# Convolution stage of a two-block transformer kernel: two alternating modulation accumulators, their column sums later, and another order of products in the first seven-product unit

## Chip, cores and metric

The kernel runs on one core of one Trainium2 chip. The metric is the device time of one execution, in microseconds (us). Engines are called PE (TensorE), ACT (ScalarE), DVE (VectorE), POOL (GpSimd) and SP (SyncE, which here only issues DMAs).

## What is computed

Two transformer blocks follow each other on 1024 rows of 1024 features, all in fp32. The first has attention and a mixture of experts. The second begins with a short convolution and ends with a gated feed forward. Only the second block's front is touched here:

```python
def second_block(x, c, ada_w, ada_b, norm_gains, conv_w_in, conv_w, conv_w_out, ...):
    c_act = jax.nn.silu(c)
    mod = c_act @ ada_w[i] + ada_b[i]                       # 6 vectors of 1024
    sh_m, sc_m, g_m, sh_f, sc_f, g_f = jnp.split(mod, 6, axis=-1)
    h = modulate(rms_norm_2(x, norm_gains[i, 0]), sh_m, sc_m)
    h = short_conv_mixer(h, conv_w_in[j], conv_w[j], conv_w_out[j])
    x = x + g_m[:, None, :] * rms_norm_2(h, norm_gains[i, 1])
    h = modulate(rms_norm_2(x, norm_gains[i, 2]), sh_f, sc_f)
    h = swiglu(h, ffn_w_gate_up[i], ffn_w_down[i])
    return x + g_f[:, None, :] * rms_norm_2(h, norm_gains[i, 3])

def short_conv_mixer(h, w_in, w_conv, w_out):
    gate_b, gate_c, v = jnp.split(h @ w_in, 3, axis=-1)
    u = gate_c * v
    conv = causal convolution of u over 3 rows, per feature
    return (gate_b * conv) @ w_out
```

The vector `mod` has 12 halves of 512 columns. Halves 0 to 3 (`sh_m`, `sc_m`) are made early in the kernel. Halves 4 to 11 (`g_m`, `sh_f`, `sc_f`, `g_f`) are made during the convolution stage, beside the product `h @ w_in`.

## The kernel before

Every fp32 operand of a matmul is split into a high and a low part (a cast on ACT, a subtraction on DVE, lines 79 and 80), and three matmuls (lines 239 to 241) make one product of the split operands.

**Seven-product units.** After a first stretch in the common form, `h @ w_in` is done in units of 256 weight columns by Winograd's form of Strassen's product (`wino`, L1538): seven products, each of 4 x 3 matmuls, called by what the weights multiply: 11, T2, T3, T1, 21, T4, 22. The weights of 11, T2, T3 and T1 are the split pair `g1` (`w_one`), those of 21, T4 and 22 the pair `g2` (`w_two`). The sums of weight blocks that they need are made on POOL (`w_sums`, L1516 to L1519). A unit's raw weights are one DMA of 1 MB (`cwraw`, issued on SP at L225). A product lands in one PSUM bank of seven (tag `pb`); ACT copies 11 (`p1c`, L1563), and DVE adds the others up (L1561). In two units of three POOL and DVE also multiply the result with an earlier factor (L1647, L1649). The row differences T1, T2, T3 are made by `wino_t` (L1479), T4 by `wino_t4`. The convolution stage has nine such units. The feed forward calls the same function for twenty units.

**Modulation beside it.** `ada_conv` (L1582) makes the eight halves in 64 steps (8 halves of 8 steps k). A step loads 256 KB of `ada_w` by a DMA on SP (L1589), scales it on ACT in place (L1597; for k = 0 into the accumulator), and adds it to the accumulator on POOL (L1599; not for k = 0). The tile `adt` (in the traces `s_st`) has four slots of 512 columns: three for raw rows, one for the accumulator. So the load of step n + 2 may go out when step n - 1 has left its slot, and the step k = 0 of the next half must wait until the column sums of the last half have read the accumulator. These column sums (`ada_finish`, L172) are four small matmuls on PE (L175) and an add on DVE (L179). In program order each product starts one step (`ada_step`, L1555), or two for 11 and 21: nine in a unit.

**Order of the work.** The program's order is a priority. A planner (the framework's scheduler, with a timing model of its own) places each instruction on its engine when it finds it ready; after that every engine, and SP's queue, is strictly in order. In the trace PE's column sums stand between matmuls 6 and 7 (twice 7 and 8) of T2, and not where the program writes them.

**After the stage.** The raw rows for the output projection (`yr`, L1683, loaded from `y_d`) take the memory of `adt`, so their load waits on SP for the last column sums. Their split (into the memory of `hh`, `hl`, which the nine units read until their end) feeds the first matmuls of the output projection (`pm`).

Of the kernel before, what the change touches and what calls it, by code (L numbers as in the profile page):

```python
# [45 lines left out]
def block_kernel(ctx: ExitStack, tc: tile.TileContext, a, out, dbg=None, upto=99):  # L46
# [35 lines left out]
    # ---------------------------------------------------------------- constants  # L82
# [18 lines left out]
    def newton_rsqrt(eng, v, n, name, iters=3):  # L101
        """rsqrt(-2v) of v < 0: y = y*(1.5 + v*y*y)"""
# [23 lines left out]
    def rstd_s(ss, n, name):  # L126
        """as rstd_of, from the square root of ACT"""
# [20 lines left out]
    # ---------------------------------------------------------------- adaptive modulation  # L148
# [4 lines left out]
    def ada_gen(pool_, which, h, eng, tags="ad"):  # L153
        """One 512-column half of the modulation vector, in steps."""
# [26 lines left out]
    # ---------------------------------------------------------------- DRAM scratch  # L181
# [25 lines left out]
    def build_h(t, src, rstd, arow, brow, tmp, hi, lo, eng=None):  # L207
        """h = src*rstd*arow + brow, transposed into the split halves of token tile t."""
        h_rows(t, src, rstd, arow, brow, tmp.tile([P, D], F32, name="hrow", tag="hrow", bufs=hb[0]), hi, lo, eng)
# [33 lines left out]
    # ================================================================ phase 1: z  # L243
# [77 lines left out]
    # shift and scale, the same row in every partition  # L321
# [25 lines left out]
    def ada_start(items):  # L347
        """the halves in turn on DVE and on ACT with Pool"""
# [23 lines left out]
    def rope(dst, src, t, nb):  # L372
        """dst, src [P, nb, 64]"""
# [10 lines left out]
    def put(hi, lo, src, scale=1.0):  # L384
        """the split halves of scale*src"""
# [3 lines left out]
    def rope4(t, pz, hi, lo, scale):  # L389
        """four rope heads of 64, transposed in pairs into the split tiles"""  # L390
# [9 lines left out]
    def ct_chunk(t, pz, hi, lo):  # L400
        """rms of the 256 columns of pz, transposed into the split tiles"""
# [103 lines left out]
    for i, (kind, c) in enumerate(chunks):  # L505
# [6 lines left out]
        if i == 1:  # L512
            # the rest of the modulation waits for the up projections
# [53 lines left out]
    # ================================================================ phase 2: attention  # L567
# [140 lines left out]
    def gate_w(raw, c):  # L708
        """gate1 goes into the columns of the projection"""
# [61 lines left out]
    # ================================================================ phase 3: out projection, router  # L771
# [80 lines left out]
    # the router works on the unnormalised row: logits = rstd*(x1 @ (a2*wr)) + (s2 @ wr + br)  # L852
# [14 lines left out]
    def router(t, xT, r):  # L867
# [43 lines left out]
        # tokens and weights of the slots, by rank and expert  # L911
# [63 lines left out]
    # the rows of ys_d that hold a token's two results: its slots, or the row of zeros if the expert was full  # L975
# [606 lines left out]
    def ada_conv():  # L1582
# [10 lines left out]
        for n_, (h, k) in enumerate(steps):  # L1593
# [7 lines left out]
            if k == KD - 1:  # L1601
                ada_finish(adt[:, 3, :], 1, h)
# [417 lines left out]
```

## Time and profile before

| What | us |
| --- | --- |
| median of three runs | 2591.1 |
| lowest and highest run | 2588.51 and 2593.97 |
| span of the profiled execution, first to last instruction | 2593.1 |
| PE busy in it | 2367.3 (91%) |
| DVE, ACT, POOL busy | 1916.8 (74%), 1213.2 (47%), 1034.5 (40%) |

The profiled execution's own time is not listed apart from its span; the span lies 2.0 us above the median of the runs and within what they cover. All times of rows are counted from the start of that span. The convolution's seven-product units run from 1572.5 to 1785.8 us, the feed forward's from about 1947 us on. A busy share is an average; what a stage is worth is read from who waits for whom in that stage.

### The profile page before, as it was taken

The page shows a single profiled execution, that of the slowest core. Times are in us where ns is not written, and L with a number is a line of the kernel's source. Part 1 is how long each engine was busy: PE and PEld are TensorE (multiplying, and loading weights), DVE is VectorE, ACT ScalarE, POOL GpSimd, SP SyncE. Part 2 cuts the span into 40 slices and gives each one's busy share as a digit, 9 for nine tenths or more (in the row PEclk, how much of TensorE's full clock was granted, in tenths as well). Part 3 has the DMA queues.
Part 4 walks back from the last instruction along what each step waited for, and adds up shares of the span by engine and source line. Part 5 has one row for each costly group of instructions (what it writes and reads, how often), then busy time and mean ns, then how long its engine had stood idle before and what let it go on. Part 6 is the DMA issues. An engine that isn't in the chain of part 4 may idle for free. (4 is left out here: it accounts for less than half of the span.)

```text
span 2593.1 us, 35011 instructions
## 1 busy us (share of the span) xinstructions
PE 2367.3 (91%) x12889; PEld 1955.1 (75%) x12889; DVE 1916.8 (74%) x2965; ACT 1213.2 (47%) x1622; POOL 1034.5 (40%) x973
## 2 busy tenths in 40 slices
PE   6998889999898899999999688899998999999986
PEld 3888768888798577766666577778986888887775
DVE  7777457777667799999999586676687555558777
ACT  3344346666522577766677443444232222223443
POOL 2644115554512221232520466883343333437143
PEclk8999999999999899999999689999998999999999
DMA  7566983331435799999998743445212222137545
GB/s 283 160 220 191 294 264 107 114 105 51 141 125 185 266 382 379 379 381 366 375 372 323 206 132 111 149 142 167 98 66 78 68 91 89 66 114 243 171 146 171
DMA packets 253379, 503.74 MB, mean 194 GB/s; under 512 B 21009, under 2 KB 99089, under 8 KB 248849
## 3 DMA queue, kind: packets, MB, share of 16 engines
q1 hardware_dynamic: 236210, 436.69, 48.7%
q0 software_dynamic: 16704, 63.71, 8.5%
q8 instruction: 102, 1.67, 0.3%
q10 hardware_dynamic: 288, 1.05, 0.1%
q14 instruction: 75, 0.61, 0.1%
HBM read 427.46 MB, written 78.13 MB: 195 GB/s over the span
## 5 line engine op out<-in xcount | busy, mean ns | idle before, releaser
L1039 DVE TENSOR_TENSOR mlo<-mraw,mhi 128x1024 fp32r<-128x1024 f32 x378 | 440.2, 1216 | 28.9 <-ACT mhi L1034 13.7
L1034 ACT CAST mhi<-mraw 128x2048 fp32r<-128x2048 f32 (+1 forms) x193 | 364.0, 1903 | 72.6 <-PE gu L241 27.8
L240 PE MATMUL gu<-mlo,xh 128*96 128x512 f32 x512 | 206.0, 402 | 10.6 <-DVE mlo L1039 10.6
L239 PE MATMUL gu<-mhi,xh 128*96 128x512 f32 x512 | 203.6, 398 | 0.0
L241 PE MATMUL gu<-mhi,xl 128*96 128x512 f32 x512 | 201.0, 393 | 0.0
L1043 POOL DMA_INDIRECT xg<-h_d,idxg x32 | 120.4, 3761 | 100.2 <-PE xT L1054 87.2
L241 PE MATMUL pz<-zhi,hlo 128*128 128x256 f32 (+1 forms) x512 | 149.7, 294 | 6.6 <-DVE hlo L80 6.6
L239 PE MATMUL pz<-zhi,hhi 128*128 128x256 f32 (+1 forms) x512 | 148.8, 295 | 7.4 <-ACT zhi L79 7.3
L1105 POOL DMA_DIRECT2D ys_d<-ysb x30 | 16.2, 541 | 336.2 <-DVE ysb L1103 329.6
L240 PE MATMUL pz<-zlo,hhi 128*128 128x256 f32 (+1 forms) x512 | 149.1, 293 | 0.6 <-DVE zlo L80 0.6
L601 PE MATMUL ps<-k,oq 128*128 128x512 f32 x416 | 127.4, 418 | 15.2 <-ACT em L608 9.7
L239 PE MATMUL wm<-hh,g2hi 128*128 128x512 f32 x348 | 135.4, 389 | 0.0
L240 PE MATMUL wm<-hl,g2hi 128*128 128x512 f32 x348 | 135.4, 389 | 0.0
L241 PE MATMUL wm<-hh,g2lo 128*128 128x512 f32 x348 | 135.4, 389 | 0.0
L606 DVE TENSOR_REDUCE nmx<-ps 128x1 f32<-128x1024 f32 x96 | 116.1, 1218 | 22.7 <-PE ps L601 22.3
L240 PE MATMUL dd<-pp 128*128 128x512 f32 x308 | 121.5, 396 | 8.9 <-DVE pp L80 8.7
L241 PE MATMUL dd<-pp 128*128 128x512 f32 x308 | 119.7, 390 | 0.0
L240 PEld LDWEIGHTS gu<-mlo,xh 128*96 128x96 f32 x512 | 82.8, 162 | 46.3 <-DVE mlo L1039 14.9
L79 ACT CAST pp<-dr 128x1024 fp32r<-128x1024 f32 x55 | 57.5, 1050 | 128.3 <-POOL dr L1852 50.1
L239 PE MATMUL dd<-pp 128*128 128x512 f32 x308 | 108.9, 396 | 8.7 <-ACT pp L79 4.5
L80 DVE TENSOR_TENSOR ptwraw<-pT,ptwhi 128x512 fp32r<-128x512 f32 x128 | 83.9, 682 | 36.9 <-ACT ptwhi L79 36.8
L239 PEld LDWEIGHTS gu<-mhi,xh 128*96 128x96 f32 x512 | 82.9, 162 | 36.3 <-ACT mhi L1034 1.2
(604 smaller groups left out, 7487.6 us busy)
## 6 DMA issues: line engine op xcount, KB each, us to landing
mraw<-in_w_expert_gate SPq DMA_DIRECT2D x64, 1024.0 KB, 16.5
mraw<-in_w_expert_up SPq DMA_DIRECT2D x64, 1024.0 KB, 17.1
mraw<-in_w_expert_down SPq DMA_DIRECT2D x64, 1024.0 KB, 15.2
fwraw<-in_ffn_w_gate_up SPq DMA_DIRECT2D x21, 1024.0 KB, 5.7
dr<-a_d SPq DMA_DIRECT2D x77, 256.0 KB, 4.3
adraw<-in_w_ada SPq DMA_DIRECT2D x64, 256.0 KB, 4.1
s_st<-in_ada_w SPq DMA_DIRECT2D x64, 256.0 KB, 2.9
dr<-in_ffn_w_down SPq DMA_DIRECT2D x55, 256.0 KB, 4.3
```

The lines of the kernel that those rows point to most:

```text
L79: act.copy(hi, src)
L80: (eng or dve).tensor_tensor(out=lo, in0=src, in1=f32(hi), op=OP.subtract)
L239: pe.matmul(ps, lhsT=lh, rhs=rh, start=first, stop=False)
L240: pe.matmul(ps, lhsT=lh, rhs=rl, start=False, stop=False)
L241: pe.matmul(ps, lhsT=ll, rhs=rh, start=False, stop=last)
L601: pe.matmul(ps[:, cs], lhsT=l, rhs=r[:, cs], start=(i == 0), stop=(i == len(passes) - 1))
L606: dve.reduce_max(nm, ps, axis=AX.X, negate=True)
L1034: act.copy(hi[:, m], raw[:, m])
L1039: eng.tensor_tensor(out=lo[:, m], in0=raw[:, m], in1=f32(hi[:, m]), op=OP.subtract)
L1043: pool.indirect_dma_start(out=xg[e % XG][:CAP], out_offset=None, in_=h2f, in_offset=bass.IndirectOffsetOnAxis(ap=idxg[:CAP, e:e + 1], axis=0),
L1105: (sp if e >= NE - 2 else pool).dma_start(ys_d[e * CAP:(e + 1) * CAP, :], y)
```

## The change

Two things are changed, and a number of comments are taken out.

First, `ada_conv`: `adt` has the same four slots, now two for raw rows and two for accumulators that alternate between halves. A step loads one step ahead where it loaded two ahead, so the load of step n + 1 may go out when step n - 1 has left its slot. The column sums of a half are written after the step k = 4 of the following half; those of the last half come at the end.

```diff
-                sp.dma_start(adt[:, n_ % 3, :], wv[:, k, h * 512:(h + 1) * 512])
+                sp.dma_start(adt[:, n_ % 2, :], wv[:, k, h * 512:(h + 1) * 512])
         load(0)
-        load(1)
         for n_, (h, k) in enumerate(steps):
-            load(n_ + 2)
-            raw = adt[:, n_ % 3, :]
+            load(n_ + 1)
+            raw, acc = adt[:, n_ % 2, :], adt[:, 2 + h % 2, :]
             sc = cg[0][:, 8 + k:9 + k]
-            act.activation(adt[:, 3, :] if k == 0 else raw, raw, AF.Copy, scale=sc)
+            act.activation(raw if k else acc, raw, AF.Copy, scale=sc)
             if k:
-                pool.tensor_tensor(out=adt[:, 3, :], in0=adt[:, 3, :], in1=raw, op=OP.add)
+                pool.tensor_tensor(out=acc, in0=acc, in1=raw, op=OP.add)
+            if k == 4 and h > 4:
+                ada_finish(adt[:, 2 + (h - 1) % 2, :], 1, h - 1)
             yield
-            if k == KD - 1:
-                ada_finish(adt[:, 3, :], 1, h)
+        ada_finish(acc, 1, h)
```

Second, `wino`: in the first unit of a call (the convolution's and the feed forward's) the order of products is 11, 21, 22, T2, T3, T1, T4. The result of 22 stays in its bank until its add at the end of the unit.

```diff
             act.copy(p1c, prod(w1, 0, "11"))
+            if i == 0:
+                ps21, ps22 = prod(w2, 0, "21"), prod(w2, 2, "22")
+                add(dst(0), ps21, p1c)
             add(u2, prod(w1, 3, "T2"), p1c)
             add(u3, prod(w1, 2, "T3"), u2)
...
-            add(dst(0), prod(w2, 0, "21"), p1c)
+            if i:
+                add(dst(0), prod(w2, 0, "21"), p1c)
             fin(0)
             add(dst(2), prod(w2, 1, "T4"), u3)
             fin(2)
-            add(dst(1), prod(w2, 2, "22"), dst(1))
+            add(dst(1), prod(w2, 2, "22") if i else ps22, dst(1))
```

## Rows read from the trace of the kernel before

**Rows 1.** The page: span, and the chain that ended last, shares by engine

```profile
span 2593.1 us, 35011 instructions
PE 15%; DVE 10%; DMA 9%; POOL 4%; issue 3%; ACT 2%; SPq 0%; DVEq 0%; POOLq 0%; ACTq 0%
```

**Rows 2.** Same chain, 1583.2 to 1793.2 us alone, shares by line

```profile
by line: DMA s_st<-in_ada_w 32.1%; POOL s_st L1599 23.4%; issue 8.4%; DMA coraw<-in_conv_w_out 7.3%; ACT s_st L1597 6.4%; POOL s_sw L1516 4.3%; POOL s_sw L1517 3.5%; DVE g2lo L80 2.2%; POOL s_uu L1647 1.9%; ACT p1c L1563 1.6%; POOL s_cc L16
```

**Rows 3.** Same chain and stretch, its longest loads of a step: start, us, what

```profile
1587.08 6.95 DMA s_st<-in_ada_w
1610.42 5.25 DMA s_st<-in_ada_w
1660.06 5.96 DMA s_st<-in_ada_w
1730.19 5.78 DMA s_st<-in_ada_w
```

**Rows 4.** Units: us, busy (x) of PE, PEld, DVE, ACT, POOL, clock, DMA

```profile
1600.40:1621.80 21.40, 20.23 (x93) 16.57 (x92) 10.64 (x13) 9.38 (x13) 15.58 (x12) 1.00 0.46 147
1621.80:1647.20 25.40, 21.90 (x94) 17.88 (x94) 21.86 (x20) 11.64 (x16) 23.73 (x14) 0.93 0.43 126
1647.20:1673.80 26.60, 22.93 (x93) 18.79 (x92) 17.45 (x17) 9.84 (x14) 21.68 (x14) 0.87 0.51 166
1673.80:1693.80 20.00, 20.00 (x93) 16.67 (x93) 9.33 (x11) 9.41 (x13) 15.57 (x13) 1.00 0.50 159
1693.80:1718.00 24.20, 21.91 (x94) 17.73 (x94) 22.52 (x19) 11.39 (x15) 23.75 (x14) 0.93 0.41 128
1718.00:1742.60 24.60, 21.81 (x94) 17.78 (x93) 16.03 (x16) 8.45 (x13) 19.02 (x12) 0.93 0.51 166
1742.60:1765.70 23.10, 21.84 (x94) 17.73 (x93) 12.34 (x16) 10.63 (x15) 18.32 (x13) 0.93 0.41 134
1765.70:1785.80 20.10, 20.10 (x93) 16.53 (x92) 14.91 (x18) 6.16 (x7) 7.48 (x5) 1.00 0.35 93
```

**Rows 5.** Waits, 1583 to 1770 us: total us, times, longest

```profile
ACT s_st L1597 <- DMA s_st<-in_ada_w: 102.6, 42, 6.0
PE adp L175 <- POOL s_st L1599: 14.7, 6, 3.7
```

**Rows 6.** Groups, 1583 to 1770 us: line, names, count, busy us, mean ns, idle before

```profile
L1599 POOL TENSOR_TENSOR s_st<-s_st 128x512 f32<-128x512 f32 x56 | 87.6, 1565 | 27.3 <-ACT s_st L1597 25.1
L1597 ACT ACTIVATE s_st<-s_st,cact 128x512 f32<-128x512 f32 x64 | 45.5, 723 | 102.8 <-DMA s_st<-in_ada_w 102.6
```

**Rows 7.** The chain in order of time, pieces of one period: start, us, what

```profile
1617.93 1.31 POOL s_st L1599
1619.24 0.02 issue
1619.26 2.89 DMA s_st<-in_ada_w
1622.15 0.02 issue
1622.18 0.73 ACT s_st L1597
...
1622.95 0.71 issue
1623.66 1.75 POOL s_st L1599
1625.41 0.02 issue
1625.43 2.83 DMA s_st<-in_ada_w
```

**Rows 8.** POOL's instructions in that period: start, us, line, names

```profile
1620.90 2.80 POOL L1647 TENSOR_TENSOR s_uu<-s_uu,s_cc 128x512 f32<-128x512 f32 x1
1623.66 1.74 POOL L1599 TENSOR_TENSOR s_st<-s_st 128x512 f32<-128x512 f32 x1
1625.37 1.26 POOL L1516 TENSOR_TENSOR s_sw<-cwraw 128x512 f32<-128x512 f32 x1
1626.60 1.71 POOL L1517 TENSOR_TENSOR s_sw<-cwraw 128x512 f32<-128x512 f32 x1
1628.27 1.26 POOL L1599 TENSOR_TENSOR s_st<-s_st 128x512 f32<-128x512 f32 x1
```

**Rows 9.** All loads of the steps, and all column sums: first and last start

```profile
L1589 SPq DMA_DIRECT2D s_st<-in_ada_w x64: 327/328/833, 1583.2 to 1760.0; - x64
L175 PE MATMUL adp<-ones,s_st x64: 164/250/370, 1605.8 to 1768.4; 128*128 128x1 f32 x64
```

**Rows 10.** After the units: `yr` from issue to landing, its split, PE's first `pm`

```profile
1768.70 0.96 SPq L1683 DMA_DIRECT2D yr<-y_d  x2
DMA to landing us min/median/max: 3.6/4.7/5.8
1793.35 0.94 DVE L80 TENSOR_TENSOR hl<-yr,hh 128x768 fp32r<-128x768 f32 x1
1788.63 0.83 ACT L79 CAST hh<-yr 128x768 fp32r<-128x768 f32 x1
1793.15 0.58 PE L241 MATMUL pm<-cohi,hl 128*128 128x256 f32 x1 [4.18 <-DVE hl L80]
```

**Rows 11.** First unit of the convolution: PE's waits, DVE's split of `g2`

```profile
1577.22 0.47 PE L239 MATMUL wm<-t2h,g1hi 128*128 128x512 f32 x1 [1.88 <-DVE s_cc L1634]
1584.44 0.77 PE L239 MATMUL wm<-t3h,g1hi 128*128 128x512 f32 x1 [4.25 <-DVE s_cc L1634]
1584.22 1.21 DVE L80 TENSOR_TENSOR g2lo<-cwraw,g2hi 128x1024 fp32r<-128x1024 f32 x1
```

**Rows 12.** First unit of the feed forward: the same

```profile
1962.55 0.79 PE L240 MATMUL wm<-t2l,g1hi 128*128 128x512 f32 x1 [4.31 <-DVE t2l L1482]
1963.55 1.21 DVE L80 TENSOR_TENSOR g2lo<-fwraw,g2hi 128x1024 fp32r<-128x1024 f32 x1
```

## Prediction

> **What bounds the kernel now.** I read the chain of waits first, whole and then cut to the changed stage, then the units, then who waits for whom there. Over the whole span PE leads the chain with 15% [rows 1]. Cut to the convolution stage it is another matter: the modulation's loads, scalings and adds hold 32.1%, 6.4% and 23.4% of the chain, and no matmul is among its leading lines [rows 2]. The stage is bound by a ring: load a quarter megabyte, scale it on ACT, add it on POOL, load again into the slot left. PE feels the ring at one place. Its column sums stand in its queue before the last add is done, and PE waits 14.7 us there in six pieces [rows 5]. The units show the price: seven units from 1600.4 to 1765.7 us take 165.3 us, where the one in which PE never waits takes 20.0 us with a granted clock of 1.00 [rows 4]. Seven of those are 140.0, so 25.3 us are lost: 14.7 in waiting, the other 10.6 in matmuls after a wait, in units whose granted clock is 0.87 to 0.93. That is what the change can win. But the longest row of the stage is a different one: ACT sits idle 102.6 us, 42 times, for the landing of a step's load, with three raw slots [rows 5].
>
> **The change, part by part. The accumulators.** Instructions are the same in number and shape: 64 loads, 64 scalings, 56 adds, eight groups of sums. What is removed is a wait: the step k = 0 of a half no longer waits for the sums of the half before. What is added is a wait too: a load goes out when the slot two steps back is left, where it was three.
>
> What does one pass of a slot cost? In the chain of one period a load goes out at 1619.26, lands at 1622.15, and is scaled by 1622.95 (3.69 us) [rows 7]. The add is 1.57 us in the mean of 56 [rows 6], the next issue 0.02 behind it. A pass is 5.28 us. A half is eight steps, so with three slots 8/3 passes, 14.1 us; with two, four passes, 21.1 us. The slot that takes the odd steps ends with the add of k = 7 and has none of the steps k = 0, so nothing is spared there.
>
> Two things lie in the way of the passes in every period. One is the 1 MB weight load of the unit: a step's load issued behind it takes 6.95, 5.25, 5.96, 5.78 us [rows 3] where others take 2.83 and 2.89 [rows 7]; 3.1 us more in the mean, once a period. The other is POOL's other work. In the period read, an add that was ready at 1622.95 started 0.71 us later behind L1647 [rows 7, 8], and the next one, whose predecessor ended at 1625.41, started at 1628.27 behind L1516 and L1517, 2.86 us later [rows 8]. Together 3.6 us of POOL.
>
> A test on the kernel before: 14.1 + 3.1 + 3.6 = 20.8 us. Measured, the eight groups of sums lie 23.1 us apart (first start 1605.8, last start 1768.4, the last being the eighth matmul of its group: some 162 us in seven periods) [rows 9]. The 2.3 us left are the wait of k = 0 for PE, which the change removes. With two slots and without that wait a period is 21.1 + 3.1 + 3.6 = **27.8 us**. The ring gets 4.7 us longer a half, not shorter.
>
> Bounds for the period: the weight load and POOL's work fully hidden give 21.1. The longest load (4.1 more) and all of POOL's other work in the way give the other end: POOL is busy 137.7 us in the seven units, of which 49 adds of 1.57 are 76.7 [rows 4, 6], so 8.7 a unit, and 21.1 + 4.1 + 8.7 = 33.9. I take 27.8, since it uses the delays read in one period of the same ring, and the same terms return 20.8 of 23.1 before.
>
> **From the ring to the end.** The ring starts with the first load at 1583.2 [rows 9], and this stays. Seven periods of 27.8 and a last one of 21.1, when the units and their loads are done, end at 1583.2 + 194.6 + 21.1 = 1798.9. Then come the last sums (about 1.1), the load of `yr`, which lies in the memory of the slots and takes 3.6 to 5.8 us, its cast and subtraction (0.83 and 0.94) and some 0.3 of handing over [rows 10]: 6.8 us with the shorter load. The first full `pm` would start at 1805.7; before it is at 1793.15 [rows 10]. From there on PE's work is unchanged, so the kernel ends **12.5 us later**. The units, which may run up to 25.3 us shorter, wait at their end for the ring: the gain is real on PE and lies beside the chain. If that cover were gone (a ring of 23 us), it would show in full.
>
> **What queues behind the new wait.** On SP a load that waits for POOL holds what is behind it: the 1 MB weights of the next unit, the stores of `y_d`, then `yr`. On ACT a scaling that waits for a landing holds the casts of `g1` and `g2` behind it, on which DVE and then PE wait. The ring's lateness so reaches PE by two more ways than the sums. I set this at nothing on the end as long as the ring ends after the units; otherwise see the third rival.
>
> **The sums half a period later.** They cost PE the same. The program's order doesn't place them: before, the program asks for nine steps a unit and the ring made eight, so the planner put the sums where it thought them ready, one group a unit [rows 9]. A slower ring falls further behind the program, and the sums may again stand at the planner's estimate. This costs nothing here, as PE is covered by the ring.
>
> **The order of products.** 21 and 22 need `g2`, whose low part DVE writes from 1584.22 us on in the convolution and from 1963.55 in the feed forward; T2 starts at 1577.22 and 1962.55 [rows 11, 12]. So 21 isn't ready when PE idles before T2, and PE's idle time there (1.88 and 4.25 us in the convolution) can't be filled unless the splits move too. The second wait, of T3, ends with the multiplication on DVE that frees the last banks of the stage before; whichever product takes that bank waits as long. In the convolution the ring covers it, -5 to +4 us on PE, nothing on the end. In the feed forward nothing covers it: 21 placed strictly ahead of T2 would wait for the 1.21 us that end at 1964.8, 2.2 us later than T2 starts; two products of 2.7 us (a seventh of the 20.0 us unit without its sums) in PE's idle time, were `g2` ready, would win 5.4. I take 0, since the planner starts whatever is ready, and keep -5.4 and +2.2 for the range. The bank that 22 holds through the first unit is the third of seven and is asked for again seven products later, in the second unit, when the add at the first unit's end is done: nothing; were it late, the most is a product's 2.7 us.
>
> **Sum.** 12.5 us on the profiled execution's span of 2593.1, which lies 2.0 above the median of 2591.1; the median after is 2591.1 + 12.5 = 2603.6 us.
>
> **A rule that speaks the other way.** ACT waits 102.6 us for loads with three slots [rows 5]. The Trainium skill (Trainium Kernel Development and Optimization, Best Practices) says to double-buffer, so that transfers overlap the work. By that rule two raw slots would do, and the time would be that of the first rival. The row speaks against it here, since three slots already leave ACT waiting.
>
> **The rivals.**
> First, faster: the ring keeps its old pace. If the period stays at 23.1 us, it ends at 1583.2 + 161.7 + 21.1 = 1766.0, the units without their 25.3 us at 1760.5, and `pm` starts at 1772.8: 20.3 us earlier, 2570.8 us. It needs POOL's other work to slip into the ring's pauses wholly, and part of the weight load besides. For it: with two slots adds come singly, and POOL has pauses between them. Against it: POOL is busy up to 23.75 of 24.2 us in some units [rows 4]. It decides from a period below 26.0 us, where (1793.15 - 6.8 - 1583.2 - 21.1)/7 lies.
> Second, no change: the period lands between 25.3 and 26.7 us, 2586 to 2596; or the sums again stop PE where the planner expected them, so that the change does not do what it says, and the faster ring's gain is eaten by the same waits.
> Third, much slower: the planner thinks the ring faster than it is and puts most of its steps ahead of the last units' casts on ACT. Then PE follows the ring, and a last unit (20.0 us) and the 7.4 us from its end to `pm` (1785.8 to 1793.15) come after the ring: 1798.9 + 20.0 + 7.4 = 1826.3, 33 us later, 2624 us. The order of ACT's queue before, where casts stand behind waiting scalings, is for it; that the ring lags the program by a step a unit is against it.
>
> **How the numbers follow.** Forecast (2596 to 2612) 0.46; third rival and what lies between 0.17; no change 0.15; faster 0.22. A difference under 0.2%, 5.2 us, can't be told from none in this kernel. Slower is 0.46 + 0.17 = 0.63. The range: below, a period of 24.1 us gives 2578, which leaves out about half of the faster case, 0.11; above, 2628 takes in the third rival with a few us of the first units and leaves out 0.06.
>
> **What would show it.** Right: in the trace after, ACT's wait for the loads is longer than 102.6 us; the eight groups of sums (or the last adds of the halves) lie 26 to 30 us apart; the last sums come near 1800 us; PE idles between the units' end and `pm`, and `yr` is issued right behind the last sums. Wrong: periods near 23 us, or a `yr` that is issued before the units end. The pass is wrong if a lone load takes much else than 2.9 us, and the order of products if PE starts 21 before 1584 us or before 1962.

## The result and the profile after

| | before | after |
|---|---|---|
| time, median (us) | 2591.9 (2588.5 to 2594.0, 4 runs) | 2616.3 (2614.4 to 2621.1, 4 runs) |
| profiled execution: time, span (us) | span 2593.1 | 2621.1, span 2619.2 |
| mean granted clock of TensorE in it | 0.959 | 0.955 |

The kernel became 24.4 us slower: ratio 1.0097, interval 1.0083 to 1.0111. The forecast was 2603.6 us, 12.5 us slower. So the direction and the mechanism that I named came true, and the size was half.

First the changed ring. The slots' tile in after: all loads of the steps and all column sums, with first and last start.

```profile
L1594 SPq DMA_DIRECT2D s_st<-in_ada_w x64: 327/328/532, 1583.5 to 1792.2; - x64
L175 PE MATMUL adp<-ones,s_st x64: 164/250/373, 1612.0 to 1802.7; 128*128 128x1 f32 x64
```

The waits of after from 1583 to 1805 us (total us, times, longest):

```profile
ACT s_st L1602 <- DMA s_st<-in_ada_w: 118.0, 47, 6.3
POOL s_st L1604 <- ACT s_st L1602: 53.3, 25, 5.2
PE adp L175 <- POOL s_st L1604: 25.8, 6, 13.6
```

The last load goes out at 1792.2 us and not at 1760.0, the last sums come at 1802.7 and not at 1768.4 [rows 9]. ACT waits 118.0 us for the loads, where it was 102.6, and PE 25.8 us ahead of its sums, where it was 14.7 [rows 5]. Of those 25.8 one piece is 13.6 us. Here it is, on PE's timeline (start, us, instruction, in brackets the idle time before it and what ended it):

```profile
1787.17 0.39 PE L241 MATMUL wm<-hh,g2lo 128*128 128x512 f32 x1
1801.20 1.87 PE L175 MATMUL adp<-ones,s_st 128*128 128x1 f32 x8 [13.64 <-POOL s_st L1604]
1802.93 1.95 PE L142 MATMUL brow<-ident,gm_c 128*128 128x128 f32 x8
1807.93 1.97 PE L142 MATMUL brow<-ident,af_c 128*128 128x128 f32 x8 [3.06 <-ACT gmrow L143]
...
1810.83 0.56 PE L241 MATMUL pm<-cohi,hl 128*128 128x256 f32 x1
```

The units end at 1787.6, then PE has nothing to do until the ring's last add. Before, the ring ended under the units. What lies behind the ring is now exposed, and most of all the eight loads of `yr`, which lie in the ring's memory. The chain of waits from 1802 to 1850 us, by line and in its longest pieces (start, us, what):

```profile
by line: DMA yr<-y_d 63.0%; DVE hl L80 12.6%; ACT hh L79 5.3%; DVE coq L80 4.7%; PE pm L239 2.9%; DVE cv L1727 2.7%; issue 2.4%; PE pm L240 2.2%; PE pm L241 1.8%; DVE cr_e L109 0.8%; SPq L1680 0.7%; DVE cr_y L114 0.7%; DVE gf_c L1334 0.4%; 
1806.09 13.38 DMA yr<-y_d
...
1821.33 4.73 DMA yr<-y_d
...
1828.52 6.13 DMA yr<-y_d
...
1836.53 5.99 DMA yr<-y_d
...
1845.24 1.29 DVE cv L1727
...
1846.67 0.55 PE pm L239
```

`yr` holds 63% of it. One load takes 13.38 us, where the longest before took 5.8 [rows 10]. ACT's and DVE's timelines show why the last of the eight matters:

```profile
1838.82 0.83 ACT L79 CAST hh<-yr 128x768 fp32r<-128x768 f32 x1 [3.31 <-DMA yr<-y_d]
1839.56 1.02 ACT L1725 ACTIVATE cv<-pm 128x1024 f32<-128x1024 f32 x1
1842.54 0.83 ACT L79 CAST hh<-yr 128x768 fp32r<-128x768 f32 x1 [1.88 <-DMA yr<-y_d]
1843.40 0.96 DVE L80 TENSOR_TENSOR hl<-yr,hh 128x768 fp32r<-128x768 f32 x1 [1.92 <-ACT hh L79]
```

Seven of the eight casts stand in ACT's queue ahead of the square of the first row tile (L1725), and the subtraction behind the eighth (L80) stands in DVE's queue ahead of `cv` (L1727). PE's third row tile, which needs the first one's bank, waits 5.16 us for that `cv`, until 1846.67.

To compare kernels I take the starts in their traces from the ring's first load on, since what lies ahead of it moves all of them by up to 11 us. `fm` is the first matmul of the feed forward. The last column is the difference of the medians within one set of runs. All times in us.

| kernel | last sums start | PE's wait ahead of them | units end | first full `pm` | last `yr` cast ends | first `fm` | median against before |
|---|---|---|---|---|---|---|---|
| before | 184.4 | 0 | 202.7 | 209.9 | 233.1 | 313.6 | |
| after | 217.7 | 13.6 | 204.1 | 227.4 | 259.9 | 339.4 | +24.4 |
| acc_only | 233.7 | 33.6 | 200.1 | 245.7 | 264.8 | 345.3 | +31.9 |
| order_only | 183.9 | 1.6 | 202.4 | 209.5 | 232.3 | 312.8 | +2.4 |
| raw2_acc1 | 239.3 | 26.6 | 197.1 | 248.2 | 270.0 | 350.4 | +35.1 |
| raw3_acc2 | 179.7 | 2.2 | 208.1 | 215.3 | 238.4 | 318.9 | +5.1 |
| after_k7 | 183.4 | 0 | 205.3 | 214.1 | 237.4 | 317.9 | +4.8 |
| after_late | 211.4 | 9.0 | 202.4 | 228.5 | 253.6 | 333.6 | +20.8 |
| raw3_late | 199.2 | 0 | 203.0 | 217.7 | 239.8 | 320.9 | +6.6 |
| after_gf_late | 218.1 | 13.5 | 204.6 | 227.7 | 256.0 | 336.1 | +22.3 |
| before_gf_late | 183.5 | 0.9 | 203.5 | 210.7 | 233.8 | 314.3 | +0.3 |
| after_yr3 | 218.7 | 13.5 | 205.2 | 222.6 | 251.0 | 332.4 | +16.1 |
| after_yr3_gf | 217.1 | 13.7 | 203.4 | 221.0 | 251.0 | 332.4 | +18.4 |
| after_gfT | 216.7 | 12.2 | 204.5 | 226.5 | 248.7 | 327.8 | +19.0 |
| before_gfT | 182.1 | 1.5 | 202.2 | 209.3 | 231.8 | 312.3 | +2.9 |
| after_yr3_gfT | 218.0 | 13.7 | 204.3 | 222.0 | 243.4 | 324.8 | +15.1 |

Read it once for the change: of the 25.8 us between 313.6 and 339.4, 1.4 lie at the units' end, 16.1 between there and the first full `pm` (23.3 where it was 7.2), and 8.3 between that and `fm` (112.0 where it was 103.7). From `fm` to the end the two traces need 696.2 and 696.3 us. What `fm` has over 313.6 agrees with the last column within 5 us in every row. The largest gaps, 3.9 to 4.8 us, are those of the three runs with `gfT`, so a difference of that size between two rows of one column proves nothing.

### The profile page after: what moved, and what is told of

Its sections match the earlier page's. It is cut to its first block, busy times and chain, and to the rows that moved or that the text cites. A ratio compares the mean times of both kernels' runs of the same rounds, so it can differ in the third digit from the quotient of the medians.

```text
span 2619.2 us, 35014 instructions
## 1 busy us (share of the span) xinstructions
PE 2372.2 (91%) x12889; PEld 1960.0 (75%) x12889; DVE 1925.5 (74%) x2965; ACT 1214.0 (46%) x1622; POOL 1040.0 (40%) x973
## 5 line engine op out<-in xcount | busy, mean ns | idle before, releaser
L1039 DVE TENSOR_TENSOR mlo<-mraw,mhi 128x1024 fp32r<-128x1024 f32 x378 | 440.2, 1216 | 28.6 <-ACT mhi L1034 13.7
L240 PE MATMUL gu<-mlo,xh 128*96 128x512 f32 x512 | 205.9, 402 | 10.5 <-DVE mlo L1039 10.5
L239 PE MATMUL gu<-mhi,xh 128*96 128x512 f32 x512 | 203.6, 398 | 0.0
L239 PE MATMUL pz<-zhi,hhi 128*128 128x256 f32 (+1 forms) x512 | 149.4, 296 | 7.8 <-ACT zhi L79 6.6
L239 PE MATMUL wm<-hh,g2hi 128*128 128x512 f32 x348 | 137.5, 395 | 16.4 <-ACT g2hi L79 15.3
L240 PE MATMUL pz<-zlo,hhi 128*128 128x256 f32 (+1 forms) x512 | 149.8, 294 | 0.6 <-DVE zlo L80 0.6
L1105 POOL DMA_DIRECT2D ys_d<-ysb x30 | 16.3, 544 | 336.1 <-DVE ysb L1103 329.5
L240 PE MATMUL wm<-hl,g2hi 128*128 128x512 f32 x348 | 136.8, 393 | 0.0
L240 PE MATMUL dd<-pp 128*128 128x512 f32 x308 | 121.8, 396 | 9.0 <-DVE pp L80 8.9
L240 PEld LDWEIGHTS gu<-mlo,xh 128*96 128x96 f32 x512 | 82.8, 162 | 46.2 <-DVE mlo L1039 14.8
L239 PE MATMUL dd<-pp 128*128 128x512 f32 x308 | 108.7, 395 | 9.1 <-ACT pp L79 4.4
L80 DVE TENSOR_TENSOR ptwraw<-pT,ptwhi 128x512 fp32r<-128x512 f32 x128 | 83.8, 681 | 37.1 <-ACT ptwhi L79 37.0
L1604 POOL TENSOR_TENSOR s_st<-s_st 128x512 f32<-128x512 f32 x56 | 88.8, 1586 | 54.3 <-ACT s_st L1602 53.3
## 6 DMA issues: line engine op xcount, KB each, us to landing
dr<-a_d SPq DMA_DIRECT2D x77, 256.0 KB, 4.1
adraw<-in_w_ada SPq DMA_DIRECT2D x64, 256.0 KB, 4.5
s_st<-in_ada_w SPq DMA_DIRECT2D x64, 256.0 KB, 2.9
dr<-in_ffn_w_down SPq DMA_DIRECT2D x55, 256.0 KB, 4.3
```

What stands on the lines that cost most here:

```text
L80: (eng or dve).tensor_tensor(out=lo, in0=src, in1=f32(hi), op=OP.subtract)
L239: pe.matmul(ps, lhsT=lh, rhs=rh, start=first, stop=False)
L240: pe.matmul(ps, lhsT=lh, rhs=rl, start=False, stop=False)
L1039: eng.tensor_tensor(out=lo[:, m], in0=raw[:, m], in1=f32(hi[:, m]), op=OP.subtract)
L1604: pool.tensor_tensor(out=acc, in0=acc, in1=raw, op=OP.add)
```

## The experiments

### Which part of the change: acc_only, order_only, raw2_acc1, raw3_acc2

**acc_only**: the accumulators without the new order of products (against the changed kernel).

```diff
-            if i == 0:
-                ps21, ps22 = prod(w2, 0, "21"), prod(w2, 2, "22")
-                add(dst(0), ps21, p1c)
...
-            if i:
-                add(dst(0), prod(w2, 0, "21"), p1c)
+            add(dst(0), prod(w2, 0, "21"), p1c)
...
-            add(dst(1), prod(w2, 2, "22") if i else ps22, dst(1))
+            add(dst(1), prod(w2, 2, "22"), dst(1))
```

> The change without its new order of products: two raw slots, two accumulators, sums half a period behind. Theory (the two raw slots alone make the loss): as the changed kernel, 2613 to 2620 us, the sums 26.5 to 27.5 us apart and the last one near 1801 us. Rival (the new order delays the first units, and half of the loss is its own): 2600 to 2608 us.

Measured 2623.2 us, ratio 1.0122 (1.0107 to 1.0137), a little more than the changed kernel. The loss is all there without the new order. The expectation of the sums was wrong: the first seven groups are 27.9 us apart ((1776.6 - 1609.0)/6), and the eighth comes 39.8 us behind the seventh, at 1816.4 us. SP's timeline (start, us, issue) shows why:

```profile
1779.93 0.38 SPq L225 DMA_DIRECT2D coraw<-in_conv_w_out  x1
1781.49 2.02 SPq L1589 DMA_DIRECT2D s_st<-in_ada_w  x2
1783.60 0.86 SPq L1712 DMA_DIRECT2D x3r<-x_d  x2
1797.14 0.38 SPq L225 DMA_DIRECT2D coraw<-in_conv_w_out  x1
1797.62 1.01 SPq L1589 DMA_DIRECT2D s_st<-in_ada_w  x2
1805.79 0.38 SPq L225 DMA_DIRECT2D ffraw<-in_ffn_w_gate_up  x1
1806.91 0.33 SPq L1589 DMA_DIRECT2D s_st<-in_ada_w  x1
```

And PE's timeline at the last sums of acc_only:

```profile
1816.36 1.87 PE L175 MATMUL adp<-ones,s_st 128*128 128x1 f32 x8 [33.62 <-POOL s_st L1599]
```

The weight loads of the next stage (`coraw`, `ffraw`) stand in SP's queue ahead of the ring's last three loads; that the planner takes the ring for faster than it is would explain it. They wait for buffers that DVE, which reads them last, frees late: SP issues nothing for 12.7 us ahead of 1797.14, and `coraw` goes out 0.03 us behind this subtraction on DVE's timeline:

```profile
1795.90 1.21 DVE L80 TENSOR_TENSOR coq<-coraw,coq 128x1024 fp32r<-128x1024 f32 x1
```

The ring's loads stand behind, and PE waits 33.6 us.

**order_only**: the same lines the other way round, the new order put into the kernel before.

> The new order of products alone, on the kernel before with its three raw slots and one accumulator. Theory (slots make the loss, the order is worth next to nothing): 2588 to 2596 us. Rival (the order costs half of the loss): 2600 to 2606 us.

Measured 2593.6 us, ratio 1.0007 (0.9996 to 1.0018). In the kernel before, the order by itself can't be told from nothing. The changed kernel is 7 us quicker than acc_only, and its last sums start 16.0 us earlier from the ring's first load on; this fits the loads that stand ahead of the ring's last ones on SP in acc_only. Whether the order has a part in it once the ring is late, no run separates.

**raw2_acc1**: two raw slots, but one accumulator and the sums at the end of each half.

```diff
-            raw, acc = adt[:, n_ % 2, :], adt[:, 2 + h % 2, :]
+            raw, acc = adt[:, n_ % 2, :], adt[:, 3, :]
...
-            if k == 4 and h > 4:
-                ada_finish(adt[:, 2 + (h - 1) % 2, :], 1, h - 1)
             yield
-        ada_finish(acc, 1, h)
+            if k == KD - 1:
+                ada_finish(acc, 1, h)
```

(against acc_only)

> Two raw slots with one accumulator, and the sums at the end of each half as before; the old order of products. Theory (the two raw slots make the ring late, the second accumulator has nothing to do with it): the ring ends no earlier than in the changed kernel, its halves 27 to 29 us apart, 2614 to 2628 us. Rival (the loss comes of the alternating accumulators and their sums half a period behind): 2588 to 2600 us.

Measured 2627.4 us, ratio 1.0132 (1.0117 to 1.0148), the sums 30.3 us apart. Against the kernel before, this run differs in the third raw slot alone, with the load two steps ahead that goes with it, and it has the whole loss: 35.1 us, with sums 30.3 us apart where they were 23.1. The lost raw slot is the loss. Against acc_only the interval overlaps (1.0107 to 1.0137), so what the second accumulator gains in time isn't shown; in the traces it brings the first seven groups from 30.6 to 27.9 us apart.

**raw3_acc2**: the slot given back. The second accumulator lies in a tile that the units use for U3; they now write U3 into the block of the result that it ends in.

```diff
-                sp.dma_start(adt[:, n_ % 2, :], wv[:, k, h * 512:(h + 1) * 512])
+                sp.dma_start(adt[:, n_ % 3, :], wv[:, k, h * 512:(h + 1) * 512])
...
-            load(n_ + 1)
-            raw, acc = adt[:, n_ % 2, :], adt[:, 2 + h % 2, :]
+            load(n_ + 2)
+            raw, acc = adt[:, n_ % 3, :], acc_of(h)
...
+    adx = pF.tile([P, 512], F32, name="adx", tag="u3")
+    acc_of = lambda h: adx if h % 2 else adt[:, 3, :]
...
-            p1c, u2, u3 = wino_tmp(pl)
+            u3 = pl.tile([P, H], F32, name="u3", tag="u3") if own3 else dst(2)
```

> Three raw slots and two accumulators with the sums half a period behind; the second accumulator lies where the convolution's units keep U3, which they now write into its block of the result. Old order of products. Theory (the third raw slot restores the ring's pace of 23 us or better, and the sums no longer hold PE): the last sums before the units' end at 1786 us, PE's waits ahead of the sums 14.7 us down to 0 to 8 us, 2575 to 2590 us. Rival (the planner and POOL set the ring's pace, not the slots): sums 26 to 28 us apart again, 2608 to 2622 us.

Measured 2597.4 us, ratio 1.0022 (1.0012 to 1.0032). One raw slot more takes the loss of acc_only from 31.9 to 5.1 us, and the sums are 22.3 us apart. This is the test that tells slots from planner and POOL: the rival's 26 to 28 us and 2608 to 2622 did not come. But I had expected it to be faster than the kernel before, and it is not. PE's waits in it, from 1585 us on:

```profile
PE adp L175 <- POOL adx L1601: 9.6, 3, 7.0
PE adp L175 <- POOL s_st L1601: 8.7, 4, 5.2
```

They come to 18.3 us, more than the 14.7 before [rows 5], though the program asks for the sums half a period later.

### Is the ring's end the cause, and do PE's waits under the units count: after_k7, after_late, raw3_late

**after_k7**: a ring shorter by an eighth; it leaves out the last of the eight row blocks of each half.

```diff
-        steps = [(h, k) for h in range(4, 12) for k in range(KD)]
+        steps = [(h, k) for h in range(4, 12) for k in range(KD - 1)]
```

> The changed kernel with a shorter ring: the second half of the modulation is summed over seven of its eight row blocks, so 8 of 64 loads, scalings and 8 of 56 additions are left out. Theory (the whole loss is that the ring ends behind the units): sums 23 to 24.5 us apart, the last ones at 1770 to 1782 us under the units' products, 2580 to 2596 us. Rival (the sums half a period behind or the new order cost the units time of their own): 2604 to 2612 us.

Measured 2597.2 us, ratio 1.0013 (1.0003 to 1.0024), 1 us above what was expected. The period is 23.1 us, and with the ring's end under the units 19.6 of the 24.4 us are gone, by the medians. The edit takes work from ACT and POOL, too; what that is worth beyond the ring's end is not separated.

**after_late**: the sums a whole half behind, and the ring spread at eight steps to a unit, so that PE meets each group at the end of the next unit.

```diff
-                ada_step(1 + (j == 0))
+                ada_step(1 + (n_ == "11"))
...
-            if k == 4 and h > 4:
+            if k == KD - 1 and h > 4:
                 ada_finish(adt[:, 2 + (h - 1) % 2, :], 1, h - 1)
             yield
+        for _ in range(7):
+            yield
         ada_finish(acc, 1, h)
```

> The changed kernel, two raw slots, with the sums placed as in the run with three slots and late sums: one half to a unit, sums at the end of the next unit. Theory (PE's waits ahead of the sums under the units cost nothing, as the ring's end decides): waits ahead of the sums but the last nearly gone, the ring ends where it did, near 1800 us, the wait ahead of the last sums is longer by what the units gain, 2612 to 2620 us. Rival (those waits are part of the loss): 2604 to 2610 us.

Measured 2614.5 us, ratio 1.0084 (1.0069 to 1.0098), as the changed kernel within what can be told. The waits ahead of the sums under the units went from 12.2 only to 9.7 us, so the run says little of them.

**raw3_late**: the same on raw3_acc2. Here the sums found their columns ready.

> Three raw slots, two accumulators (memory as in the run with three and two), one step of the ring at each product and a second one at each unit's first product, so one half to a unit, and the sums of a half a whole half behind, at the end of the next unit. Old order of products. Theory (what is left in the kernel before is PE's wait of 14.7 us ahead of sums that the planner places at its own, too early, estimate of POOL's end; placed a unit later they find their columns ready): waits ahead of the sums 0 to 5 us, 2578 to 2588 us. Rival (what PE gains there it loses elsewhere, to the units' operands, the granted clock or the yr loads): 2590 to 2600 us.

Measured 2600.3 us, ratio 1.0024 (1.0011 to 1.0036). The rival holds. PE's waits from 1585 us on:

```profile
PE wm L239 <- ACT g1hi L79: 13.2, 4, 5.6
PE pm L239 <- ACT hh L79: 7.7, 1, 7.7
```

No wait ahead of sums is left, and in their place stand 13.2 us for the high parts of the next unit's weights, which are loaded and cast late. The longest of the four, on ACT's timeline:

```profile
1644.93 0.72 ACT L1599 ACTIVATE s_st<-s_st,cact 128x512 f32<-128x512 f32 x1 [4.10 <-DMA s_st<-in_ada_w]
1646.59 0.72 ACT L1599 ACTIVATE s_st<-s_st,cact 128x512 f32<-128x512 f32 x1 [0.93 <-DMA s_st<-in_ada_w]
1647.21 0.60 ACT L79 CAST g1hi<-cwraw 128x512 fp32r<-128x512 f32 x1
```

These weights landed at 1644.26 us, and ACT casts them 2.95 us later, behind two scalings that wait for their loads; their own load had gone out only at 1637.54. The units end at 203.0 us where they ended at 202.7, so nothing of the 14.7 us that PE waits for sums in the kernel before was won by this placement: the weights of the next units come next. Another placement wasn't tried. The 6.6 us by which the run is slower lie behind the units: its last sums start 14.8 us later than before, `yr` waits for them, and the first full `pm` starts 7.8 us later.

### What lies behind the ring: after_gf_late, before_gf_late, after_yr3, after_yr3_gf, after_gfT, before_gfT, after_yr3_gfT

The traces show one suspect in both kernels. `gf_c`, 128 partitions by 8 numbers, is written to `gf_d` in 4-byte packets. The DMA view of after from 1800 to 1830 us, the throughput in forty slices of 0.75 us each, the packets by size, and the write (count, KB, us to landing):

```profile
GB/s 274 382 385 176 0 33 191 283 19 22 15 0 0 3 57 22 28 11 4 17 12 38 38 78 302 360 366 363 335 294 258 280 74 19 0 0 0 130 303 385
DMA packets 6724, 4.17 MB, mean 139 GB/s; under 512 B 1136, under 2 KB 6723, under 8 KB 6723
...
gf_d<-gf_c SPq DMA_DIRECT2D x1, 4.0 KB, 9.7
```

The same view of before from 1770 to 1800 us:

```profile
GB/s 143 315 334 191 21 65 288 369 386 299 9 0 0 0 0 0 0 0 0 0 8 87 162 284 367 388 377 418 421 208 76 0 99 274 237 274 206 264 279 340
```

In after the write is issued at 1805.67 us; from 1806 to 1818 the core moves at most 78 GB/s and mostly under 25. In before it is issued at 1776.15, and from 1778.25 to 1785.0 nothing moves; in the first 3.7 us of that SP has issued nothing else, in the rest a load of `coraw` waits. That the mechanism was there before, too, and that its place has changed, is what makes it a suspect: before, a load of `coraw` fell into it (issued at 1781.94, landed at 1791.26), and now a load of `yr`.

**after_gf_late, before_gf_late**: this DMA moved in the program to the end of the out projection.

```diff
-    sp.dma_start(gf_d.rearrange("o (k p) -> p (o k)", p=P), gf_c)
...
         co_tile(t, pm)
+    sp.dma_start(gf_d.rearrange("o (k p) -> p (o k)", p=P), gf_c)
     st7.close()
```

> The changed kernel with one DMA moved: the write of gf_c to gf_d, 1024 packets of 4 bytes, goes from ahead of the yr loads to behind the eight row tiles of the out projection. Theory (this write holds up the queue for 8 to 10 us, and in the changed kernel the exposed yr loads stand behind it): the 13.4 us load of yr comes down to 4 to 5 us, 2604 to 2609 us. Rival (the yr loads are slow for a reason of their own, the sixes of row pieces or the first reads of y_d): 2614 to 2618 us, a yr load of over 10 us stays.

> The kernel before with the same DMA moved. Theory (its stall falls there on loads that lie under the units' products or have time): 2588 to 2592 us, no more than 3 us gained. Rival (the stall costs there as much as in the changed kernel, so it is no part of the difference): 2580 to 2584 us.

Measured 2613.6 us, ratio 1.0079 (1.0064 to 1.0094), and 2591.6 us, ratio 0.9999 (0.9990 to 1.0008). Neither answers anything, since the planner has not followed the edit. In before_gf_late the write goes out 192.0 us behind the ring's first load, where it was 192.9, between the same two loads of `coraw`. SP's timeline of after_gf_late:

```profile
1804.93 0.96 SPq L1688 DMA_DIRECT2D yr<-y_d  x2
1807.47 0.36 SPq L1759 DMA_DIRECT2D gf_d<-gf_c  x1
1810.67 0.37 SPq L225 DMA_DIRECT2D ffraw<-in_ffn_w_gate_up  x1
1811.91 1.66 SPq L1688 DMA_DIRECT2D yr<-y_d  x2
1826.29 0.37 SPq L225 DMA_DIRECT2D fwraw<-in_ffn_w_gate_up  x1
```

The write is issued at 1807.47, behind the second `yr` and ahead of the others; the hold-up has only passed to the third and fourth, issued at 1811.91 and 1813.22; in the chain of waits the fourth takes 12.46 us.

**after_yr3**: a third place for `yr`, outside the ring's memory.

```diff
+    yr0 = pG.tile([P, 6, P], F32, name="yr0")
+    yrs = [yr0, yr[:, 0], yr[:, 1]]
-        sp.dma_start(yr[:, t % 2], y_d[:, :, ts].rearrange("k p n -> p k n"))
-        split(h2h[:, 0:6, ts], h2l[:, 0:6, ts], yr[:, t % 2])
+        sp.dma_start(yrs[t % 3], y_d[:, :, ts].rearrange("k p n -> p k n"))
+        split(h2h[:, 0:6, ts], h2l[:, 0:6, ts], yrs[t % 3])
```

> The changed kernel with a third place for yr, outside the ring's memory: the first yr load no longer waits for the ring's end, the other seven go through three places and not two. Theory (what the loss has beyond the ring's 13.6 us is the chain of eight yr casts, which all stand on ACT ahead of the first row tile's square): the last yr cast 8 to 15 us earlier than 1843 us, 2603 to 2609 us. Rival (the rows after the ring cost the same, whatever yr does): 2613 to 2619 us.

Measured 2608.4 us, ratio 1.0065 (1.0043 to 1.0086): 8.3 us come back of 24.4. So the rows behind the ring do cost, beside PE's wait.

**after_yr3_gf**: both edits.

> The changed kernel with both edits behind the ring: the third place for yr, and the 4-byte write of gf_d behind the out projection's row tiles. Theory (with one of them alone the other still holds the row tiles: 8 us and 3 us came back singly, PE waited 6.4 us more behind a 13.4 us load in the first): 2599 to 2605 us, what is left is the ring's 13.5 us ahead of the last sums. Rival (the write's stall is covered once the places are three): 2606 to 2611 us.

Measured 2612.0 us, ratio 1.0070 (1.0057 to 1.0083), no better than the third place alone, and 1 us above the rival's range. Again the planner issued the write at 1805.13 us among the `yr` loads, and a wait of 8.3 us of PE for `afrow`, which ACT copies behind a `yr` cast, stayed. The longest `yr` load takes 15.8 us in it. The combination was not tested by it.

**after_gfT, before_gfT, after_yr3_gfT**: the hold-up taken away itself. PE transposes `gf_c`, and eight rows of 512 bytes are written.

```diff
-    sp.dma_start(gf_d.rearrange("o (k p) -> p (o k)", p=P), gf_c)
+    ptg = ptb("gfT")
+    pe.transpose(ptg[0:KD, 0:P], gf_c, ident)
+    gft = const.tile([P, P], F32, name="gft", tag="diag", bufs=2)[0:KD]
+    dve.tensor_copy(gft, ptg[0:KD, 0:P])
+    sp.dma_start(gf_d.rearrange("o (k p) -> (o k) p", p=P), gft)
```

> The changed kernel with gf_c transposed by PE ahead of its write, so that gf_d is written in 8 packets of 512 bytes and not in 1024 of 4 bytes. Theory (the 4-byte write holds the queue for 8 to 10 us, and the exposed yr loads stand behind it): no yr load over 7 us, the last yr cast at 1830 to 1837 us and not at 1843 us, 2604 to 2611 us. Rival (the yr chain is slow of itself, two places and eight passes): a yr load of over 10 us stays, or the last cast comes as late without it, 2613 to 2619 us.

> The kernel before with the same 512-byte write. Theory (the hold-up falls there under the units' last products and on a weight load with time to spare, and costs little): 2587 to 2592 us. Rival (it costs there as much as in the changed kernel, 8 us, and is no part of the difference): 2580 to 2585 us.

> The changed kernel with the third place for yr and the 512-byte write. Theory (the rows behind the ring are then as quick as before, and only PE's wait of 13.5 us ahead of the last sums is left): PE's wait on afrow (6.4 and 8.3 us with the third place and the 4-byte write) below 2 us, 2599 to 2606 us. Rival (the 4-byte write costs nothing beyond what the third place gave back): 2607 to 2612 us.

Measured 2608.8 us, ratio 1.0081 (1.0065 to 1.0096); 2592.7 us, ratio 1.0003 (0.9989 to 1.0017), 0.7 us above what was expected; 2604.9 us, ratio 1.0064 (1.0047 to 1.0080). The tile `yr` in after: idle time of its engines for the load, and from issue to landing.

```profile
  DMA yr<-y_d: 19.1, 6
DMA to landing us min/median/max: 3.5/5.9/13.4
```

The same of after_gfT:

```profile
  DMA yr<-y_d: 5.3, 5
DMA to landing us min/median/max: 3.4/4.4/6.1
```

And of after_yr3_gfT:

```profile
  DMA yr<-y_d: 5.9, 4
DMA to landing us min/median/max: 3.6/4.9/6.9
```

The long loads are gone, and with them 10.2 us between the ends of the last `yr` cast in the traces (259.9 less 248.7, less 1.0 that the ring ended earlier) and 7.5 of the 24.4 us in the medians by 2616.3 and 2608.8, 5.4 by each one's own runs of before. In after_gfT the write goes out behind the second load, as in after_gf_late, with six of the eight behind it, so its packets and not its place made them long. In after_yr3_gfT the planner issues it behind the seventh load, so there both have changed.

In the kernel before the same edit changes nothing in time: the write goes out 23.7 us later there, the `coraw` load that took 9.3 us takes 5.2, and the units end as before (202.2 and 202.7).

With both edits what is left is 15.1 us by the medians and 11.2 by the traces (324.8 less 313.6). Of the 11.2, 10.5 lie between the units' end and the first full `pm` (17.7 where it was 7.2), and there PE waits 13.7 us ahead of the last sums; behind it nothing is left (102.8 us to `fm`, 103.7 before). So the account of the 24.4 us is: 11 to 15 for the ring's end, and 9 to 11 by the medians, 14.6 by the traces, for the rows behind it. Of those the write alone is 5 to 8 by the medians and the two places of `yr` alone 8, so they overlap.

## Why the prediction was wrong in size, step by step

Counted from the ring's first load, the change costs 25.8 us in the traces. 12.5 were forecast. Of the rest, 4.9 lie ahead of the first full `pm` (2.0 in the ring's end, 2.9 between it and `pm`) and 8.3 behind it.

- **The pass and the period: right.** 27.8 us were forecast, from a pass of 5.28, the weight load and POOL. Measured are 27.0 us in the mean of seven periods between the groups of sums ((1801.2 - 1612.0)/7). raw3_acc2 has 22.3 us with the third slot, so that the count of slots sets the period is shown. The size of a slot is shown, too: the passes gave 7.0 us between two slots and three (21.1 less 14.1), and raw2_acc1 and the kernel before, which differ in that alone, are 7.2 apart (30.3 and 23.1). Of the two terms that lie in the way of the passes, one was too small and one too large. Followed step by step through the trace of after, in the mean of the second to the seventh half, adds wait 5.0 us for POOL in four passes (3.6 forecast), and from issue to scaling four passes take 2.1 us more than four loads of 2.86 (3.1 forecast). That the sum came out is in part luck.
- **The ring's end: right by two errors.** 1798.9 was forecast for the last add; it ended at 1801.1. Seven halves, from the first load to the seventh group of sums, took 190.6 us (1774.1 - 1583.5) and not 194.6, and the eighth 27.1 (to 1801.2) and not 21.1. I had it free of the units' loads and POOL's sums of weights, but the next stage's work takes their place. ACT's timeline:

```profile
1793.89 1.32 ACT L79 CAST hh<-s_cc 128x256 fp32r<-128x256 f32 x4 [2.56 <-POOL s_cc L1655]
1795.12 1.04 ACT L79 CAST coq<-coraw 128x1024 fp32r<-128x1024 f32 x1
1796.06 0.72 ACT L1602 ACTIVATE s_st<-s_st,cact 128x512 f32<-128x512 f32 x1
1797.90 0.72 ACT L1602 ACTIVATE s_st<-s_st,cact 128x512 f32<-128x512 f32 x1
```

  Casts of `coraw` (to `coq`) and `s_cc` stand among the last scalings. The load of the seventh step landed at 1794.2 and was scaled at 1796.06.
- **From the ring's end to the first full `pm`: 6.8 forecast, 9.7 measured** (1801.1 to 1810.8). The sums took 1.87 us and not 1.1, and the `brow` products 1.95 and 1.97: PE came out of 13.6 us of idle time at a granted clock of 0.50, the lower level of 1.2 GHz. And ACT had two casts of `coraw` (1805.41 to 1807.4) and the copies of `gmrow`, which depends on the last sums as `yr` does, ahead of the first cast of `yr` at 1808.26; PE waited 3.06 us for `gmrow` too. I had followed one of the things behind the ring. The window of after behind the sums (us, busy us and instructions of PE, PEld, DVE, ACT, POOL, clock, DMA share, GB/s):

```profile
1803.00:1810.00 7.00, 3.94 (x19) 3.54 (x19) 5.84 (x10) 4.26 (x6) 0.00 (x0) 0.50 0.28 60
```

- **"From there on PE's work is unchanged": this is the step that failed**, 8.3 us by the traces. I took one `yr` load as the cost of what lay behind the ring. There are eight of them through two places, all in the ring's memory. Seven casts stand in ACT's queue ahead of the first row tile's square, not all eight as I wrote for after_yr3; the eighth holds `cv` by its subtraction on DVE. Before, the chain began at 1768.7 under the units, and its first two loads had 17 us of cover [rows 10]; afterwards it begins at 1803.1 without cover, and the 4-byte write falls among its loads. Of the 8.3 us, 6.0 are idle time of PE (8.1 us between `pm` and `fm`, where it was 2.0). In the other 2.3 PE is busy longer: the granted clock of this stretch is 0.93, where it was 0.98. The row was at hand: two `yr` loads issued at 1768.70, ahead of the units' end. I used it for the time of a load, and not for the cover that goes.
- **What PE gains under the units: 25.3 us were forecast, 0 came** (units end at 202.7 and 204.1 us). It cost nothing here because the ring covers it, as I had said. But it was wrong to call it a gain: no run shows one. The sums stayed where the planner thinks POOL is done (12.2 us of waits under the units, 14.7 before), as my paragraph on the sums allowed; and where raw3_late took the waits away, the weights of the next units came out as next. My test that would have shown it, the casts queued behind waiting scalings, stood in my third rival.
- **The order of products: 0 was right, its reason not.** I expected the planner to start what is ready, so that T2 would stay ahead of 21. It did start 21 first, in both units; in the convolution at 1582.32, ahead of the 1584 that I had named as the sign of an error. Two readings were wrong. 21's first matmuls (L239, L240) need the high part of `g2` alone and don't wait for the low part. And the row at 1962.55 [rows 12] is T2's second matmul: its first had started at 1957.44, behind a wait of 7.67 us. The 2.2 us of the range rest on that row. The feed forward's first unit in after (PE's timeline):

```profile
1984.79 0.79 PE L239 MATMUL wm<-hh,g2hi 128*128 128x512 f32 x1 [8.56 <-ACT g2hi L79]
...
1990.09 0.80 PE L239 MATMUL wm<-t2h,g1hi 128*128 128x512 f32 x1 [3.22 <-DVE s_cc L1785]
```

  PE waits 8.56 us for `g2hi` and 3.22 for the bank that L1785 frees, 11.8 us, where it waited 7.67 and 4.31 for T2's two parts before, 12.0 us. There the wait changes its owner and hardly its length. In the convolution it is 6.71 us for `g2hi` and 1.13 for the bank that DVE frees, 7.8 us in place of 6.1 (1.88 and 4.25) [rows 11]; in after the ring covers it, and order_only shows nothing in time.
- **The rivals.** The third one gave 2624 us by a mechanism (units that follow the ring) that did not come: the units end at their old time. Most of the loss beyond 12.5 us came from behind the ring instead. acc_only shows a relative of it that I did not see, the next stage's loads ahead of the ring's last ones on SP. The faster one needed a period below 26.0, and it was 27.0.

What stays open: why raw3_acc2 and after_k7, whose rings end under the units, are 4 to 5 us slower than before. In both traces the units end later, by 5.4 and 2.6 us. In raw3_acc2 3.7 of the 5.4 are longer waits for sums, and the rest is the same matmuls taking 1.6 us more; why the sums wait longer, I have not followed, nor after_k7.

## What to carry to other kernels

When a ring of loads is bound by its slots, price a slot by the pass (issue to landing, scaling, add, next issue) times the steps, and do it before trading a slot for a shorter wait elsewhere: here a slot was worth 27 us (acc_only against raw3_acc2) to 35 us (raw2_acc1 against the kernel before), and the one run without the waits won nothing. When the end of something moves past what covered it, list everything that waits for its memory or its result down to the last one, and look what those will now meet in the queues; the first of them alone gave half of the loss. And an edit of program order is no experiment under a planner until the trace shows that the order has changed.

## What the hardware showed that I had not expected

A write of 4 KB in packets of 4 bytes took 9.7 us to land, and the loads issued beside it waited. In after the throughput falls from over 280 to below 80 GB/s for 12 us while loads are under way, and a `yr` load of 384 KB takes 13.4 us, where the longest before took 5.8. In before a `coraw` load beside the write takes 9.3 us, and 5.2 in before_gfT. Written as eight rows of 512 bytes the same data delay nothing that the traces show (longest `yr` load 6.1 us in after_gfT, 6.9 in after_yr3_gfT). The Trainium skill (DMA: Bandwidth & Descriptors, Rules for kernel authors) says that a strided last dimension becomes one descriptor for each element and advises to rearrange; the trace agrees on the packets (1136 of them under 512 B in the window above), and adds that other loads of the queue pay.
